# Row sums of the softmax taken from a column of ones beside the values, in a two-layer hybrid attention kernel

## The chip, the cores and the metric

The kernel runs on one core of a Trainium2 chip. The metric is the device time of one execution in microseconds (us); lower is better. The core has a tensor engine (PE, with its weight loads shown as PEld), a vector engine (DVE), a scalar engine (ACT), GpSimd (POOL), and SP, which issues the DMAs. Each engine takes its instructions in order from a queue of its own; semaphores tie the queues together.

## The reference, cut to what matters

Two layers. Each projects the normed input once, runs three kinds of attention on the columns, gates the result and projects it back:

```python
def hybrid_layer(x, ...):
    h = rms_norm(x, g_pre)
    a_q, a_kv, a_g, b_cq, b_ckv, b_kr, c_q, c_kv, z = split_cols(h @ w_in)
    o_a = nsa_attention(...)            # 4 heads: compressed + selected + window 512, sigmoid gates
    o_b = causal_block_attention(...)   # 4 heads, latent keys and values, full causal
    o_c = banded_attention(...)         # 8 heads, window 128, with a sink for each head
    mixed = concatenate([o_a, o_b, o_c]) * silu(z)
    return x + rms_norm(mixed @ w_out, g_post)
```

Every attention is, for each head and each tile of 128 queries, `softmax(q k^T * scale + bias) @ v` with head size 64. The softmax divides by the sum of its row; with sinks, `exp(sink - max)` is added to that sum. There are 1024 tokens, so 8 tiles of queries. With 1024 tokens and 16 blocks of 64, the selected attention selects every block, so the kernel computes it as causal attention.

## The kernel before, in words

Arithmetic: float32 operands are carried as two float16 parts, hi and lo, and a product of two such operands is three float16 matmuls, listed in `HL` as (weights part, values part): (hi, hi), (hi, lo), (lo, hi). `split` makes the parts: an ACT copy for hi (L119), a DVE operation for lo (L120).

Each layer has four stages. `first` makes the keys and values of the banded heads (`L.V`, filled at L415) and of the compressed blocks (`L.VM`, in `compressed`). The second runs the banded heads (kind "swa") with the pieces of `second` as filler on the tensor engine; `second` also fills the latent values `L.VB` (L508). The third runs the three branches of the sparse attention (kinds "cmp", "slc", "win"), with the gate columns (L293, L571) as filler. The last, `last_phase`, runs the latent heads (kind "mla") with the output projection (L911).

The work of attention is cut into units (class `Unit`). A unit is one tile of queries of one head (of two heads for swa and cmp). It goes through three steps, a few units apart:

- `score`: matmuls into a PSUM tile psS (L619, L634, L659); a DVE operation `ttr` that adds the bias and takes the row's extreme (L577, tile mx); then `expo` on ACT, in place (L580). `expo` gives `accum_out=sm`, so ACT also writes the row's sum into the tile sm.
- `turn`, one or two units later: the weights are transposed. Early tiles go through the tensor engine (L698) and are split from PSUM. Where `by_dma` holds, they are split first, into a staging buffer of which there is one for slc (written as sz or HT in the trace), one for win (KC), a few for the others, and a DMA transposes them (L167).
- `values`, two to four units later: L710 multiplies the turned weights by the values, three matmuls of 64 columns for each block of 128 keys, into the PSUM tile psO. psO has one buffer, shared by all groups of units.

After the last unit of a group an end step divides. `end_swa` (two units): `es` = exp of sink against max (L722, L723), sum (L724), reciprocal (L726), scale by the constant OSCALE (L727), product with psO (L728) into the place of the tile's queries in QC. `end_win` (five units, six columns: cmp, slc, win of two heads): reciprocal (L735), gates and OSCALE (L736), product (L739), and then two POOL additions (L742, L743), the last into the place of the queries in QA. `end_mla` (four units): L749, L750 and four products (L753) into the gate tile sz.

A layer has 32 swa units with two exponentials each, 16 cmp units with two, and 32 each of slc, win and mla with one: 192 exponentials, 384 in the kernel. It has 16 swa, 16 win and 8 mla end steps: 80 in the kernel.

The code is written for the tile framework, which sets the semaphores, gives a tile its place when the earlier tile with the same tag is released, and places each engine's instructions at build time by a plan of its own. An engine's order is thus not the order of the source: in the trace, one group of 24 filler matmuls of L293 can have the six matmuls of a cmp unit between its third and its fourth. The tag "V" holds `L.V` and, at the end of a layer, one of the two turned mixed tiles (`mts`, L828).

Of the kernel before, what the change touches and what calls it, by code (L numbers as in the profile page):

```python
# [11 lines left out]
F16 = mybir.dt.float16  # L12
F32 = mybir.dt.float32
# [16 lines left out]
OSCALE = 1.0 / (SP * SQ)  # L30
# [38 lines left out]
def rope_rows():  # L69
    """Cosines and signed sines, for four heads of 32 channels and for halves of the tokens."""  # L70
# [20 lines left out]
def trunk(ctx, tc, a, out):  # L91
# [9 lines left out]
    def view(base, off, shape, dtype):  # L101
        """Words off... of a tile, as another shape and type."""
# [22 lines left out]
    class Ring:  # L125
        """Runs of words of a tile, taken in turn."""
# [15 lines left out]
        def done(self):  # L142
            """The oldest run may be written again."""
            self.live.pop(0)
# [5 lines left out]
    # constants  # L150
# [61 lines left out]
    def split_half(l, g, h, hi, lo):  # L212
        """Half of a group of weights as hi and lo parts."""
# [30 lines left out]
    def normed(hT, xt, xn, gpre, t, hl=None):  # L244
        """A tile of tokens, normed, into its place in the transposed h."""
# [18 lines left out]
    def first_norm(hT):  # L264
        """The transposed h of the first layer."""
# [11 lines left out]
    # ------------------------------------------------------------------ pieces of a layer  # L277
# [3 lines left out]
    def project(L, wh, sub, c, p):  # L281
        """512 tokens of 128 channels."""
# [13 lines left out]
    def split_w(l, g, base=None):  # L296
        """A group of weights as hi and lo parts, in a slot of its own or in base."""
# [5 lines left out]
    def parts_of(L, p, scale=SEVAC):  # L303
        """hi and lo parts of 512 columns of p."""
# [5 lines left out]
    def all_parts(L, p, c):  # L310
        """hi and lo parts of both halves of the tokens, once the second is there."""
# [20 lines left out]
    def turned(u, us, v, vs, table):  # L332
        """Rows us of u turned by their partners, rows vs of v."""
# [6 lines left out]
    def latent_tile(L, p, n, xn):  # L340
        """n channels of a tile of tokens, normed but for the gains."""
# [10 lines left out]
    def compress(L, l, w0):  # L352
        """The blocks of k_cmp and of v_cmp, through their small networks."""
# [32 lines left out]
    def compressed(L):  # L386
        """The blocks of k_cmp and of v_cmp, from the hidden layers of their networks."""
        hid, w2 = L.hid, L.w2
        L.KM = sb([128, 2, 64], F16, "KM")
        L.VM = sb([128, 2, 2, 64], F16, "VM")  # L390
        nc.vector.memset(L.VM, 0.0)
        p = ps("T")
# [4 lines left out]
        for half in range(2):  # L397
            r = slice(64 * half, 64 * half + 64)
            split(p[r, 128:192], SQ, L.VM[r, half, 0], L.VM[r, half, 1])

    def first(L, l, wv):
        """Keys and values of the banded heads, and the queries of four heads."""
# [62 lines left out]
    def second(L, l):  # L465
        """The other queries, and what the latents give; pieces, with their time on the tensor engine."""
# [35 lines left out]
        L.VB = sb([128, 2, NT, 256], F16, "VB")  # L502
        for t in range(NT):
# [4 lines left out]
            split(p[:, :256], SEVAC, L.VB[:, 0, t], L.VB[:, 1, t])  # L508
# [45 lines left out]
    def gate_path(L, l):  # L554
        """z, still without its SiLU, to DRAM; the last columns of the later tiles come with the next phase."""
# [19 lines left out]
    # ------------------------------------------------------------------ attention  # L575
# [466 lines left out]
```

## Time and profile before

| | before |
|---|---|
| time, median of 3 runs | 1182.82 us (1179.52 to 1184.2) |
| span of the profiled execution | 1186.3 us |
| instructions in the span | 25317 |
| PE, PEld busy | 86%, 56% |
| DVE, ACT, POOL busy | 65%, 60%, 9% |
| mean granted TensorE clock | 0.966 of full speed |

The span is from the first to the last instruction of one execution, taken with the profiler; what lies around it is not shown. It is 3.5 us over the median of the timed runs. Busy shares are averages over stages. Matmuls are pipelined and each is shown with its whole latency, so a PE shown as busy can still be waiting a little.

### The profile page before, as it was taken

The numbers are of one execution on the slowest core, as the hardware profiler recorded it, in microseconds if no ns is written. First come the engines' busy times: TensorE is split into PE (matmuls) and PEld (weight loads), VectorE is DVE, ScalarE is ACT, GpSimd is POOL, SyncE is SP. The second block draws the span as 40 slices with busy tenths as digits, with TensorE's granted clock in tenths as the row PEclk, the third lists the DMA queues.
The fourth block names the chain that finished last, engine by engine and source line by source line (L and its number), as shares of the span: only waits on it lengthen the run. The fifth ranks groups of instructions, "written<-read, shape, count | busy, mean of one in ns | idle before, by whom it ended". The sixth has DMA issues, their size and how long they took to land.

```text
span 1186.3 us, 25317 instructions
## 1 busy us (share of the span) xinstructions
PE 1023.0 (86%) x9536; PEld 666.9 (56%) x9536; DVE 766.7 (65%) x2268; ACT 707.9 (60%) x1659; POOL 104.7 (9%) x166
## 2 busy tenths in 40 slices
PE   6969898899888887889979989888997888789977
PEld 4535656658666663445645465664685666534443
DVE  6453677746776775678755356766576777757762
ACT  6442675647665678676744256655575667767651
POOL 1000100001100002111100010000010010021010
PEclk9989999999998997999999999999999999889989
DMA  6784475672587786555476436758327876869882
GB/s 241 172 253 115 119 152 111 131 180 66 128 147 134 132 186 201 143 121 129 112 191 186 112 90 130 147 99 176 106 80 138 163 139 128 221 148 187 186 192 89
DMA packets 313498, 174.42 MB, mean 147 GB/s; under 512 B 273580, under 2 KB 289324, under 8 KB 313376
## 3 DMA queue, kind: packets, MB, share of 16 engines
q1 hardware_dynamic: 313376, 172.81, 63.8%
q8 instruction: 75, 1.23, 0.4%
q14 instruction: 47, 0.39, 0.1%
HBM read 76.63 MB, written 21.41 MB: 83 GB/s over the span
## 4 chain that ended last, share of the span: by engine, by line
PE 30%; DMA 14%; DVE 7%; issue 5%; ACT 4%; POOL 2%; SPq 0%; POOLq 0%; ACTq 0%; DVEq 0%
PE psJ L911 11%; PE psJ L286 8%; DMA arena<-sz 4%; PE psJ L293 3%; DMA arena<-ringS 3%; PE psS L659 2%; PE psO L710 2%; DMA V<-ringS 2%; DMA arena<-KC 2%; DMA sz<-gate_rows 1%; PE psT L698 1%; DVE arena L577 1%; DMA ringS<-in_w_out_dram 1%; DVE sz L120 1%; DVE W L120 1%
## 5 line engine op out<-in xcount | busy, mean ns | idle before, releaser
L580 ACT ACTIVATE arena<-arena,mx 128x256 f32<-128x256 f32 (+8 forms) x384 | 226.4, 590 | 88.5 <-DVE mx L577 86.2
L293 PE MATMUL psJ<-W,HT 128*128 128x256 f16 x1920 | 246.1, 276 | 0.8 <-DVE VB L120 0.8
L293 PEld LDWEIGHTS <-HT 128*128 128x128 f16 x2304 | 217.5, 99 | 34.0 <-issue 6.6
L286 PE MATMUL psJ<-HT,W 128*128 128x512 f16 x864 | 198.4, 383 | 12.5 <-DVE R L120 10.6
L710 PEld LDWEIGHTS <-arena 128*128 128x128 f16 x2964 | 122.5, 99 | 80.0 <-DMA arena<-sz 42.1
L710 PE MATMUL psO<-V,arena 128*128 128x64 f16 x2304 | 106.8, 194 | 43.6 <-DMA arena<-sz 33.0
L286 PEld LDWEIGHTS <-W 128*128 128x128 f16 x864 | 83.9, 99 | 107.4 <-DVE R L120 11.5
L577 DVE CUSTOM_DVE_ANT_0 arena<-psS,R 128x64 f32<-128x64 f32 (+4 forms) x192 | 87.3, 465 | 51.9 <-PE psS L659 26.6
L120 DVE SCALAR_TENSOR_TENSOR sz<-arena,sz 128x512 f16<-128x512 f32 (+4 forms) x96 | 76.6, 801 | 45.5 <-ACT sz L119 44.6
L119 ACT ACTIVATE sz<-arena 128x512 f16<-128x512 f32 (+4 forms) x96 | 68.4, 717 | 39.6 <-DMA arena<-sz 38.4
L659 PE MATMUL psS<-KA,QA 128*128 128x512 f16 (+3 forms) x384 | 80.6, 315 | 1.5 <-DVE mx L577 1.2
L577 DVE CUSTOM_DVE_ANT_0 arena<-psS,arena,nsink 128x256 f32<-128x256 f32 (+1 forms) x128 | 57.9, 461 | 22.2 <-PE psS L634 21.3
L580 ACT ACTIVATION_READ_ACCUMULATOR arena<-arena,mx 128x1 f32 x384 | 72.3, 188 | 0.0
L911 PEld LDWEIGHTS <-arena 128*128 128x128 f16 x384 | 37.9, 104 | 57.7 <-DMA arena<-ringS 11.9
L911 PEld LDWEIGHTS <-V 128*128 128x128 f16 x384 | 36.7, 100 | 56.8 <-DMA V<-ringS 14.6
L120 DVE SCALAR_TENSOR_TENSOR arena<-psT,arena 128x128 f16<-128x128 f32 (+3 forms) x144 | 60.8, 431 | 11.7 <-ACT arena L119 10.7
L120 DVE SCALAR_TENSOR_TENSOR W<-ringS,W 128x1024 f16<-128x1024 f32 x48 | 58.5, 1222 | 14.8 <-ACT W L119 14.4
L698 PE MATMUL psT<-ident,arena 128*128 128x128 f32 x300 | 57.9, 288 | 11.5 <-ACT arena L580 10.0
L659 PE MATMUL psS<-KB,QB 96*128 96x512 f16 (+3 forms) x288 | 60.2, 337 | 2.5 <-DVE mx L577 2.5
L119 ACT ACTIVATE arena<-psT 128x128 f16<-128x128 f32 (+3 forms) x144 | 53.5, 384 | 14.8 <-PE psT L698 12.5
L171 POOL TENSOR_TENSOR rs<-rs,halfneg 128x1 f32<-128x1 f32 x48 | 26.4, 550 | 396.3 <-DVE rs L170 285.0
L911 PE MATMUL psJ<-R,arena 128*128 128x512 f16 x192 | 52.9, 432 | 9.2 <-DMA arena<-ringS 9.2
(152 smaller groups left out, 1598.7 us busy)
## 6 DMA issues: line engine op xcount, KB each, us to landing
ringS<-in_w_in_dram SPq DMA_DIRECT2D x40, 512.0 KB, 4.6
gate_rows<-sz SPq DMA_DIRECT2D x32, 256.0 KB, 3.6
ringS<-in_w_out_dram SPq DMA_DIRECT2D x16, 512.0 KB, 7.2
sz<-gate_rows SPq DMA_DIRECT2D x16, 512.0 KB, 4.2
R<-in_x_dram SPq DMA_DIRECT2D x8, 512.0 KB, 4.4
ringS<-in_cmp_w_dram SPq DMA_DIRECT2D x8, 512.0 KB, 4.8
x<-in_rope_dram SPq DMA_DIRECT2D x8, 512.0 KB, 6.2
x<-in_x_dram SPq DMA_DIRECT2D x8, 512.0 KB, 3.8
```

The source lines that it names most:

```text
L119: nc.scalar.activation(hi, src, AF.Copy, scale=scale)
L120: nc.vector.scalar_tensor_tensor(lo, src, scale, hi, op0=OP.mult, op1=OP.subtract)
L171: nc.gpsimd.tensor_tensor(dst, dst, half_neg[:, :n], op=OP.pow)
L286: nc.tensor.matmul(p, w[:, x, k, sub * 128:(sub + 1) * 128], L.hT[:, y, k, c * 512:(c + 1) * 512], start=(k == 0 and i == 0), stop=(k == K ...
L293: nc.tensor.matmul(p, L.hT[:, y, k, t * 128:(t + 1) * 128], w[:, x, k, :width], start=(k == 0 and i == 0), stop=(k == KT - 1 and i == 2))
L577: nc.vector.tensor_tensor_reduce(o, i0, i1, -alpha, init, OP.add, OP.min, acc)
L580: nc.scalar.activation(b, b, AF.Exp, bias=mx, scale=-1.0, accum_out=sm)
L659: nc.tensor.matmul(p[:, :n], q, k[:, k0 * 128:k1 * 128], start=(i == 0), stop=(i == len(pairs) - 1))
L698: nc.tensor.transpose(p[:, i * 128:(i + 1) * 128], u.b[:, (g + i) * 128:(g + i + 1) * 128], ident)
L710: nc.tensor.matmul(g["O"][:, key * 64:(key + 1) * 64], u.pt[:, x, i, :], v[:, y], start=(key not in seen and j == 0), stop=(last[key] == n ...
L911: nc.tensor.matmul(p, g["mt"][:, x, k], wo[k // 2][:, w, k % 2, cs], start=(k == 0 and i == 0), stop=(k == KT - 1 and i == 2))
```

## The change

`expo` no longer has `accum_out`, and the tile sm is gone. Every head's 64 values get a 65th column: the hi part holds the constant SQ (16) there, so the product with the weights gives the row's sum times SP times SQ, the same scale as the other 64 columns. The sums are read from psO. The (hi, lo) matmul keeps 64 columns; the other two have 65. Outputs of the heads now begin 65 words apart in psO. The column is set by POOL in `L.V` (three memsets of 8 elements a partition) and `L.VB` (four), right after the tile is taken, and by DVE in `L.VM` (two memsets); `split` then writes the values through a pattern with pitch 65. In the end steps the constant OSCALE falls away. The rest of the diff drops docstrings and comments.

```diff
-        L.VM = sb([128, 2, 2, 64], F16, "VM")
+        L.VM = sb([128, 2, 2, 65], F16, "VM")
         nc.vector.memset(L.VM, 0.0)
+        for half in range(2):
+            nc.vector.memset(L.VM[64 * half:64 * half + 64, half, 0, 64:], SQ)
...
+    def ones_of(v, n):
+        for k in range(n):
+            nc.gpsimd.memset(v[:, 0, :, 65 * k + 64:65 * k + 65], SQ)
...
-        L.V = sb([128, 2, NT, 192], F16, "V")
+        L.V = sb([128, 2, NT, 195], F16, "V")
+        ones_of(L.V, 3)
...
-            split(p[:, :192], SEVAC, L.V[:, 0, t], L.V[:, 1, t])
+            v = L.V[:, :, t].rearrange("p s (k d) -> p s k d", d=65)[:, :, :, :64]
+            split(p[:, :192].rearrange("p (k d) -> p k d", d=64), SEVAC, v[:, 0], v[:, 1])
...
-        L.VB = sb([128, 2, NT, 256], F16, "VB")
+        L.VB = sb([128, 2, NT, 260], F16, "VB")
+        ones_of(L.VB, 4)
...
-    def expo(b, mx, sm):
-        nc.scalar.activation(b, b, AF.Exp, bias=mx, scale=-1.0, accum_out=sm)
+    def expo(b, mx):
+        nc.scalar.activation(b, b, AF.Exp, bias=mx, scale=-1.0)
...
+    def sums(p, n):
+        v = p[:, :65 * n].rearrange("p (k d) -> p k d", d=65)
+        return v[:, :, :64], v[:, :, 64]
...
                 for j, (x, y) in enumerate(HL):
-                    nc.tensor.matmul(g["O"][:, key * 64:(key + 1) * 64], u.pt[:, x, i, :], v[:, y],
+                    n_ = 65 - y
+                    nc.tensor.matmul(g["O"][:, key * 65:key * 65 + n_], u.pt[:, x, i, :], v[:, y, :n_],
...
         def end_swa(u):
-            nc.vector.tensor_add(sm, sm, e)
-            nc.vector.reciprocal(rc[:, :4], sm)
-            nc.vector.tensor_scalar(rc[:, :4], rc[:, :4], OSCALE, None, op0=OP.mult)
+            nc.vector.scalar_tensor_tensor(rc[:, :4], e, SP * SQ, sm, op0=OP.mult, op1=OP.add)
+            nc.vector.reciprocal(rc[:, :4], rc[:, :4])
...
         def end_win(u):
-            nc.vector.reciprocal(rc, g["sm"])
-            nc.vector.scalar_tensor_tensor(rc, rc, OSCALE, L.G[:, u.qt, 3 * h0:3 * h0 + 6], op0=OP.mult, op1=OP.mult)
+            o, sm = sums(g["O"], 6)
+            nc.vector.reciprocal(rc, sm)
+            nc.vector.tensor_tensor(rc, rc, L.G[:, u.qt, 3 * h0:3 * h0 + 6], op=OP.mult)
...
         def end_mla(u):
-            nc.vector.reciprocal(rc[:, :4], g["sm"][:, :4])
-            nc.vector.tensor_scalar(rc[:, :4], rc[:, :4], OSCALE, None, op0=OP.mult)
+            o, sm = sums(g["O"], 4)
+            nc.vector.reciprocal(rc[:, :4], sm)
```

## Rows read from the trace of the kernel before

**Rows 1.** The busy time of the engines over the span, from the first part of the page.

```profile
PE 1023.0 (86%) x9536; PEld 666.9 (56%) x9536; DVE 766.7 (65%) x2268; ACT 707.9 (60%) x1659; POOL 104.7 (9%) x166
```

**Rows 2.** The span cut into stages: start and end, length, then busy us and instructions of PE, PEld, DVE, ACT, POOL, the granted clock, the DMA share and GB/s. In order: swa, sparse and last stage of the first layer, the same of the second.

```profile
115.00:259.00 144.00, 127.45 (x1186) 84.01 (x1185) 100.02 (x332) 87.44 (x261) 8.79 (x16) 0.99 0.63 134
259.00:447.00 188.00, 161.99 (x1997) 127.51 (x1996) 132.89 (x444) 125.76 (x330) 18.37 (x32) 0.98 0.66 135
447.00:611.00 164.00, 143.40 (x1083) 79.99 (x1082) 114.04 (x291) 108.95 (x190) 23.19 (x30) 0.95 0.59 147
...
692.00:842.00 150.00, 131.95 (x1199) 86.28 (x1197) 101.36 (x338) 89.37 (x268) 8.79 (x16) 0.97 0.60 129
842.00:1027.00 185.00, 160.10 (x2002) 126.52 (x2000) 133.36 (x445) 126.50 (x329) 18.90 (x32) 1.00 0.68 142
1027.00:1186.30 159.30, 130.78 (x923) 64.76 (x922) 91.78 (x245) 89.63 (x145) 20.45 (x24) 0.90 0.72 161
```

**Rows 3.** What PE waited for over the whole span: total us, times, longest.

```profile
PE psO L710 <- DMA arena<-sz: 33.0, 31, 2.5
...
PE psT L698 <- ACT arena L580: 10.0, 9, 2.6
PE psO L710 <- DMA arena<-KC: 9.3, 13, 1.8
...
PE psS L619 <- POOL QA L743: 6.2, 10, 1.1
...
PE psS L634 <- DVE QC L728: 1.9, 2, 1.0
...
PE psO L710 <- DVE sz L753: 0.9, 1, 0.9
...
PE psO L710 <- DVE QC L728: 0.3, 2, 0.2
PE psO L710 <- DVE tmp L739: 0.3, 1, 0.3
```

**Rows 4.** ACT in order of time, in the sparse stage of the second layer: start, length, instruction.

```profile
926.65 0.33 ACT L580 ACTIVATE arena<-arena,mx 128x64 f32<-128x64 f32 x1
926.88 0.19 ACT L580 ACTIVATION_READ_ACCUMULATOR arena<-arena,mx 128x1 f32 x1
926.98 0.33 ACT L580 ACTIVATE arena<-arena,mx 128x64 f32<-128x64 f32 x1
...
931.52 0.94 ACT L580 ACTIVATE arena<-arena,mx 128x768 f32<-128x768 f32 x1 [0.93 <-DVE mx L577]
932.37 0.18 ACT L580 ACTIVATION_READ_ACCUMULATOR arena<-arena,mx 128x1 f32 x1
932.58 0.84 ACT L119 ACTIVATE sz<-arena 128x768 f16<-128x768 f32 x1
```

**Rows 5.** Groups of one shape on ACT: count, busy us, mean ns.

```profile
L580 ACT ACTIVATION_READ_ACCUMULATOR arena<-arena,mx 128x1 f32 x384 | 72.3, 188 | 0.0
```

**Rows 6.** Pieces of the chain that ended last which lie on L580, the first and the last that hold an accumulator read; "x4" is two exponentials with their reads. The chain is shown back to 459.7 us.

```profile
694.65 0.88 ACT arena L580 x4
...
1031.21 0.61 ACT arena L580 x2
```

**Rows 7.** Groups of one shape on DVE: the end steps, and the same kind of operation with an input in PSUM and without.

```profile
L753 DVE SCALAR_TENSOR_TENSOR sz<-psO,rc,sz 128x64 f32<-128x64 f32 x64 | 14.4, 276 | 5.3 <-ACT sz L885 3.0 <-PE psO L710 2.2
...
L735 DVE RECIPROCAL rc<-sm 128x6 f32<-128x6 f32 x32 | 6.0, 188 | 4.0 <-ACT arena L580 3.8
...
L736 DVE SCALAR_TENSOR_TENSOR rc<-rc,G 128x6 f32<-128x6 f32 x32 | 5.5, 171 | 0.7
L727 DVE TENSOR_SCALAR rc<-rc 128x4 f32<-128x4 f32 x32 | 5.3, 166 | 0.5
...
L724 DVE TENSOR_TENSOR sm<-sm,es 128x4 f32<-128x4 f32 x32 | 4.9, 154 | 3.3 <-ACT es L723 3.3
...
L335 DVE TENSOR_TENSOR tmp<-psJ,x 128x512 f32<-128x512 f32 x4 | 2.8, 692 | 0.4
...
L337 DVE TENSOR_TENSOR tmp<-tmp 128x512 f32<-128x512 f32 x4 | 2.7, 685 | 0.0
```

**Rows 8.** Two groups of PE: the products with the values, and the only matmuls of 65 columns, whose moving rows lie 65 elements apart.

```profile
L710 PE MATMUL psO<-V,arena 128*128 128x64 f16 x2304 | 106.8, 194 | 43.6 <-DMA arena<-sz 33.0 <-DMA arena<-KC 9.3 <-ACT arena L119 0.3
...
L381 PE MATMUL psJ<-R,arena 128*128 128x65 f16 x192 | 6.4, 194 | 0.0
```

**Rows 9.** All engines in order of time around the end of a group in the sparse stage, tile 4 of the second layer.

```profile
911.16 0.56 DVE L739 TENSOR_TENSOR tmp<-psO,rc 128x384 f32<-128x384 f32 x1 [1.02 <-PE psO L710]
...
911.80 0.97 POOL L742 TENSOR_TENSOR tmp<-tmp 128x128 f32<-128x128 f32 x1 [9.00 <-DVE tmp L739]
...
912.85 0.45 POOL L743 TENSOR_TENSOR QA<-tmp 128x128 f32<-128x128 f32 x1
...
913.36 0.23 PE L619 MATMUL psS<-KM,QA 128*128 128x64 f16 x2 [1.14 <-POOL QA L743]
```

**Rows 10.** PE and DVE in order of time around the end of another group of that stage.

```profile
949.78 0.60 PE L293 MATMUL psJ<-W,HT 128*128 128x256 f16 x4
950.50 0.33 PE L710 MATMUL psO<-VM,arena 128*128 128x64 f16 x6
...
949.90 0.55 DVE L739 TENSOR_TENSOR tmp<-psO,rc 128x384 f32<-128x384 f32 x1
```

**Rows 11.** The border between the layers: the last product that reads the turned tile in V, the first write of the second layer's values, and POOL.

```profile
609.46 2.75 PE L911 MATMUL psJ<-W,V 128*128 128x512 f16 x12
...
614.55 0.32 ACT L119 ACTIVATE V<-psJ 128x192 f16<-128x192 f32 x1
...
615.27 0.55 POOL L923 TENSOR_TENSOR rs<-rs,halfneg 128x1 f32<-128x1 f32 x1 [13.18 <-DVE rs L922]
619.59 0.55 POOL L171 TENSOR_TENSOR rs<-rs,halfneg 128x1 f32<-128x1 f32 x1 [3.77 <-DVE rs L170]
```

**Rows 12.** Groups of one shape: a copy to strided and one to contiguous places on ACT, then memsets on POOL and DVE.

```profile
L119 ACT ACTIVATE R<-psJ 64x256 f16<-64x256 f32 x16 | 6.2, 386 | 9.3 <-DVE R L120 4.6 <-PE psJ L286 4.5
...
L119 ACT ACTIVATE VB<-psJ 128x256 f16<-128x256 f32 x16 | 5.9, 371 | 1.2 <-PE psJ L506 1.2
...
masks.py:197 POOL MEMSET ident<- 128x128 f32 x1 | 0.2, 205 | 0.3 <-POOLq L1032 0.3
...
L391 DVE MEMSET VM<- 128x128 uint32 x2 | 0.3, 165 | 0.0
```

More of the change, by code (lines that the diff above doesn't have):

```diff
@@ L29 @@
 ALPHA_B = 96.0 ** -0.5 / (SQ * SQ)
-OSCALE = 1.0 / (SP * SQ)
 NC_CMP = T // 16 - 1
@@ L398, in compressed @@
             r = slice(64 * half, 64 * half + 64)
-            split(p[r, 128:192], SQ, L.VM[r, half, 0], L.VM[r, half, 1])
+            split(p[r, 128:192], SQ, L.VM[r, half, 0, :64], L.VM[r, half, 1, :64])
+    def ones_of(v, n):
+        for k in range(n):
+            nc.gpsimd.memset(v[:, 0, :, 65 * k + 64:65 * k + 65], SQ)
     def first(L, l, wv):
@@ L507, in second @@
                                  start=(k == 0), stop=(k == 2))
-            split(p[:, :256], SEVAC, L.VB[:, 0, t], L.VB[:, 1, t])
+            v = L.VB[:, :, t].rearrange("p s (k d) -> p s k d", d=65)[:, :, :, :64]
+            split(p[:, :256].rearrange("p (k d) -> p k d", d=64), SEVAC, v[:, 0], v[:, 1])
             yield 0.4
@@ L601, in score @@
                 g["mx"] = sb([128, 8], F32, "mx", 4)
-                g["sm"] = sb([128, 6], F32, "sm", 4)
-            mx, sm = g["mx"], g["sm"]
+            mx = g["mx"]
             qs = slice(qt * 128, (qt + 1) * 128)
@@ L620, in score @@
                     ttr(b[:, r], p[:, r], cm[:, h], ALPHA, BIGF, mx[:, 3 * j:3 * j + 1])
-                    expo(b[:, r], mx[:, 3 * j:3 * j + 1], sm[:, 3 * j:3 * j + 1])
+                    expo(b[:, r], mx[:, 3 * j:3 * j + 1])
                     u.pv.append((0, 3 * j, L.VM[:, j]))
@@ L636, in score @@
                     ttr(b[:, r], p[:, r], L.stC[:, h, 256 - nk:], ALPHA, L.nsink[:, h:h + 1], mx[:, col:col + 1])
-                    expo(b[:, r], mx[:, col:col + 1], sm[:, col:col + 1])
+                    expo(b[:, r], mx[:, col:col + 1])
                     for i in range(nk // 128):
-                        u.pv.append((len(u.pv), col, L.V[:, :, k0 + i, 128:192]))
+                        u.pv.append((len(u.pv), col, L.V[:, :, k0 + i, 130:195]))
                 return
@@ L674, in score @@
                 for k in range(k0, k1):
-                    v = L.VB[:, :, k, h * 64:(h + 1) * 64] if kind == "mla" else L.V[:, :, k, w * 64:(w + 1) * 64]
+                    v = L.VB[:, :, k, h * 65:(h + 1) * 65] if kind == "mla" else L.V[:, :, k, w * 65:(w + 1) * 65]
                     u.pv.append((len(u.pv), col, v))
@@ L682, in score @@
                 init = acc
-            expo(b[:, :c], mx[:, col:col + 1], sm[:, col:col + 1])
+            expo(b[:, :c], mx[:, col:col + 1])
         def turn(u):
@@ L719, in end_swa @@
             h0 = u.h // 4 * 4
-            sm, mx = g["sm"][:, :4], g["mx"][:, :4]
+            o, sm = sums(g["O"], 4)
+            mx = g["mx"][:, :4]
             e = sb([128, 4], F32, "es", 2)
@@ L723, in end_swa @@
             nc.scalar.activation(e, e, AF.Exp)
-            nc.vector.tensor_add(sm, sm, e)
             rc = sb([128, 6], F32, "rc", 3)
-            nc.vector.reciprocal(rc[:, :4], sm)
-            nc.vector.tensor_scalar(rc[:, :4], rc[:, :4], OSCALE, None, op0=OP.mult)
-            nc.vector.tensor_tensor(own(L.QC, h0, 4, u.qt), g["O"][:, :256].rearrange("p (k d) -> p k d", d=64),
+            nc.vector.scalar_tensor_tensor(rc[:, :4], e, SP * SQ, sm, op0=OP.mult, op1=OP.add)
+            nc.vector.reciprocal(rc[:, :4], rc[:, :4])
+            nc.vector.tensor_tensor(own(L.QC, h0, 4, u.qt), o,
                                     rc[:, :4].unsqueeze(2).to_broadcast([128, 4, 64]), op=OP.mult)
@@ L748, in end_mla @@
             rc = sb([128, 6], F32, "rc", 3)
-            nc.vector.reciprocal(rc[:, :4], g["sm"][:, :4])
-            nc.vector.tensor_scalar(rc[:, :4], rc[:, :4], OSCALE, None, op0=OP.mult)
+            o, sm = sums(g["O"], 4)
+            nc.vector.reciprocal(rc[:, :4], sm)
             for h in range(4):
                 s = sz[:, 256 + h * 64:256 + (h + 1) * 64]
-                nc.vector.scalar_tensor_tensor(s, g["O"][:, h * 64:(h + 1) * 64], rc[:, h:h + 1], s,
-                                               op0=OP.mult, op1=OP.mult)
+                nc.vector.scalar_tensor_tensor(s, o[:, h], rc[:, h:h + 1], s, op0=OP.mult, op1=OP.mult)
     BY_DMA = {"cmp": NT, "slc": 3, "win": 3, "swa": 1, "mla": 0}
```

3 lines of the change are left out of this document (1 added, 2 removed).

## The prediction

> **What bounds the kernel now.** I read the engines' busy time first: PE 86% of the 1186.3 us span, DVE 65%, ACT 60% [rows 1]. ACT, which the change relieves, is not the bound on average, so the next view is the span cut by stage [rows 2]. ACT is busiest in the two sparse stages, 125.76 of 188 us and 126.50 of 185 (67 to 68%), where PE has 162 and 160; nowhere does it come above PE. So a saving on ACT counts only where something waits for ACT. The list of PE's waits says where [rows 3]. Its largest entries are the weights that a DMA turns, 33.0 + 9.3 us; those follow ACT indirectly, since ACT and DVE must split the weights before the DMA. ACT's exponential itself stands there with 10.0 us in 9 waits. The end steps stand there too, small so far: L743 on POOL 6.2 us in 10 waits, L728 1.9 and 0.3, L739 0.3, L753 0.9.
>
> In the sparse stage each unit runs in a circle: score on PE, L577 on DVE, the exponential, then on the same ACT queue the split of an earlier unit, the lo part on DVE, the DMA, values on PE, and then PE's next score. The accumulator read stands between an exponential and the split behind it [rows 4]: it is on that circle, but once for a circle of several units.
>
> **What it removes.** There are 384 accumulator reads of 188 ns, 72.3 us of ACT busy time [rows 5]. That is not what ACT's queue gets back. A read starts 0.10 us before its exponential ends, and the next instruction 0.09 us before the read ends: exponential at 926.65, read at 926.88, next exponential at 926.98, which is the first one's end [rows 4]. If the next instruction overlaps an exponential as the read does, it starts about 0.10 us sooner. So the queue gets at most 384 x 0.10 = 38 us, and whoever waits for an exponential gets 0.10 to 0.19 us.
>
> How much of the 38 us reaches the end? Two counts. Along the chain that ended last, between 459.7 us and the end, I find 18 reads, from 694.65 to 1031.21 [rows 6]; 18 x 0.10 = 1.8 us, and as much again for the other half of the 384, which lies before: 3.6 us. By PE's waits: 9 for the exponential at 0.19 = 1.7 us, and 44 (31 + 13) for turned weights [rows 3], of which I give every second one 0.10 us (the split behind a read, as at 932.58 in [rows 4], and not one that found ACT idle): 2.2 us. Together 3.9. I take a gain of 4 us; its bounds are 0 and 38.
>
> Off DVE go L724 (154 ns x 32), L727 (166 x 32) and L750 (x 16); L736 becomes a plain product. They are short and DVE has a third of its time free [rows 1, 7]. Nothing counted.
>
> **What it adds on PE.** Of 3360 matmuls on L710, two in three get one column more. The trace holds 192 matmuls of 65 columns with rows at pitch 65, as the values will lie: 6.4 us / 192 = 33 ns each, and a latency of 194 ns, the same as the 64-column matmul [rows 8], whose own share is 106.8 / 2304 = 46 ns. Zero, then. What these rows do not show is an output that starts at an odd word of PSUM, as every second head's now will.
>
> [...]
>
> **What it moves: the end steps.** This is where a price can come from. Before, the reciprocals read sm, which the exponentials wrote long before the products were done; they were over when the last matmul on psO landed, and only L739, L728 or L753 came behind. Now they read psO. Behind the last matmul come a reciprocal (L735, 188 ns) and a product (about L736, 171) before L739; a sum and a reciprocal (about 171 + 173) before L728; a reciprocal before L753 [rows 7]. With the step between two dependent DVE instructions I set 0.43, 0.43 and 0.22 us. DVE is in order, so the next unit's L577 and lo part queue behind; POOL's L742 and L743 start later by as much; and psO, which has one buffer, is released later for the next group's first product.
>
> Reading PSUM instead of SBUF I cost at nothing: the same product of 512 columns takes 692 ns with psJ as an input and 685 with SBUF alone [rows 7]. [...] The rows show 7 ns, and go into the sum.
>
> Who waits? In 10 cases PE waits for L743 already [rows 3], as at 913.36, where L739, L742 and L743 follow each other and PE stands 1.14 us [rows 9]: 10 x 0.43 = 4.3 us. Five more waits are for L728 (four) and L739 (one): 5 x 0.43 = 2.2; one for L753: 0.2. Sum 6.7 us. The bounds are 0, where the planner puts filler matmuls into the gap, and all 80 groups: 32 x 0.43 + 32 x 0.43 + 16 x 0.22 = 31 us. I take half of 6.7, that is 3.3 us, since in the later tiles PE goes on to wait for turned weights, and a PE that comes later waits less there.
>
> **What else it adds.** Fourteen POOL memsets of 8 elements; the nearest row is 128x128 in 205 ns, so under 3 us on an engine that is 9% busy [rows 1, 12]. In the second layer the first three come when the last product has read the old tile of tag V, at about 612 us; POOL is idle from there to 615.27, and the first write of V comes at 614.55 [rows 11]. Three of about 0.2 us fit. If the plan puts them behind POOL's L923 or L171 instead, that write and the second pair of input products wait until 615.9 or 620.2: up to 5 us, once. Four DVE memsets, each below the 165 ns of [rows 12], are under 0.7 us, in a stage with DVE free. The splits of V and VB write with gaps: the strided copy takes 386 ns, the contiguous one 371 [rows 12]; 32 x 15 ns = 0.5 us, beside PE work.
>
> **The sum.** 1186.3 - 4.0 + 3.3 = 1185.6 us of span. The timed median stands 3.5 us below the profiled span, so 1182.1 us; I say 1182.
>
> **The rivals.**
>
> - *ACT's queue is what paces the sparse stage.* For: the split of the weights starts right behind a read [rows 4], and PE loses 42 us waiting for what follows it [rows 3]. Against: ACT is a third idle there [rows 2], and of the waits of the exponential many are for DVE (0.93 us at 931.52). If all 192 reads of the sparse stages counted, 19 us less and 3.3 more: 1167; half of it gives about 1176.
> - *psO held longer paces PE instead.* Where the next group's product sits right behind L739, the 0.43 us fall on PE. In [rows 10] L739 ends at 950.45 and the next group's first matmul starts at 950.50, though the four filler matmuls before it had begun at 949.78; PE's list of waits does not count this, since a matmul's latency covers the gap. If all 32 sparse groups pay, 13.8 us less 4: 1193. It decides from the point where the filler before the next product is shorter than 0.43 us of PE. The stall at the border of the layers would add 5.
> - *The odd starts in PSUM cost.* If they make the write of every second head take as long again, 1680 x 33 ns = 56 us on PE: 1235. [...]
> - *A new plan.* Instructions are placed at build time, so other orders on all engines can shift the time by some us either way. It widens each case and has no sign.
>
> **How the numbers follow.** About 0.5% (5.9 us) is what a measurement of this kernel can tell from no change. The forecast, gain and price that nearly cancel, 0.39, with 1177 to 1188 as its own range. ACT as the pace, in part or whole, 0.33; psO or the border as the pace, 0.25; PSUM starts 0.03. Nearly all of the second case lies beyond 0.5%, some of the third does not: faster 0.34, same 0.39, slower 0.27. The range goes to 1167 on the one side and to 1196 on the other (1193 and part of the border's stall), which leaves the full sums of several cases and the PSUM case outside.
>
> **What would show it.** The 384 reads are gone and ACT's busy time falls from 707.9 us by 38 (if overlaps are counted once) to 72. L710 keeps its 46 ns; if it rises, the PSUM rival holds. L735 stands after the last L710 of its group, with DVE idle before it, and L739 about 0.43 us later. PE's waits on L743, L728 and psO grow by less than 7 us, and those on turned weights do not fall by more than 5. If they fall by 15, the first rival was right; if PE's waits on the end steps grow by over 10, the second. The forecast is wrong if the sparse stages change by more than 5 us each.

## The result, and the profile after

The changed kernel takes 1195.74 us (median of 4, 1194.76 to 1197.92) against 1181.87 us of the kernel before on the same chip: a ratio of 1.0122, with a 95% interval of 1.0085 to 1.0159. It is 14 us slower. The two profiled executions are closer, 1193.0 against 1186.3 us of span.

The engines' busy time, to be read against [rows 1]:

```profile
PE 1030.0 (86%) x9536; PEld 671.9 (56%) x9536; DVE 756.2 (63%) x2224; ACT 675.8 (57%) x1275; POOL 98.7 (8%) x180
```

ACT lost its 384 reads and 32.1 us of busy time, DVE 10.5 us, and PE, which bounds the kernel, gained 7. There is less work on ACT and DVE, and the kernel is slower: the loss must lie in the order, in waiting or in the clock.

The span by stage, with the columns of [rows 2], cut as near to the same work as the new order allows (PE's count differs by up to 29 in the last two stages):

```profile
112.40:260.50 148.10, 130.45 (x1185) 85.41 (x1184) 98.81 (x316) 82.39 (x197) 8.73 (x16) 0.97 0.63 130
260.50:446.00 185.50, 160.82 (x1996) 127.06 (x1995) 130.35 (x444) 119.34 (x231) 15.15 (x33) 1.00 0.68 141
446.00:608.70 162.70, 144.16 (x1084) 79.95 (x1083) 112.54 (x285) 105.12 (x161) 22.79 (x34) 0.95 0.55 142
689.00:837.40 148.40, 130.07 (x1199) 85.94 (x1197) 99.91 (x322) 84.28 (x202) 8.73 (x16) 0.98 0.60 131
837.40:1025.70 188.30, 162.74 (x1975) 128.43 (x1973) 127.52 (x434) 116.84 (x227) 16.69 (x34) 0.97 0.66 138
1025.70:1193.00 167.30, 134.21 (x952) 66.49 (x949) 93.52 (x248) 88.45 (x121) 18.98 (x23) 0.88 0.68 154
```

Against [rows 2] the stages changed by +4.1, -2.5, -1.3, -1.6, +3.3 and +8.0 us. The two layers run the same code, yet one swa stage lost 4 and the other gained 2. One profile can't carry more than that: the change is not a fixed price per group, as the kernel now stands.

The three stages that got longer are the three whose granted clock is lower than before (0.99 to 0.97, 1.00 to 0.97, 0.90 to 0.88); in the others it is equal or higher. The four timed runs of the changed kernel had a mean granted clock of 0.961 to 0.965, and the kernel before takes longer at such a clock too: of its 79 runs beside the experiments, the 11 below 0.965 took 1185.6 us in the mean, the 39 at 0.969 and above 1179.0. With 1181 us as the middle of these runs, an estimate is that up to 4 of the 14 us go with the clock. Whether the change itself brings the lower clock is not shown.

What PE waited for (total us, times, longest), against [rows 3]:

```profile
PE psO L725 <- DMA arena<-sz: 29.7, 26, 2.8
...
PE psO L725 <- DMA arena<-KC: 11.4, 12, 2.6
PE psS L633 <- POOL QA L758: 9.2, 16, 1.0
PE psS L673 <- DVE mx L587: 8.9, 8, 3.2
...
PE psO L725 <- DVE sz L768: 2.3, 4, 0.9
...
PE psO L725 <- DVE tmp L755: 1.6, 6, 0.5
```

Here L725 is the former L710, L751 to L755 the former L735 to L739, L758 the former L743. The waits on the end steps grew by 3.0 us (L758), 1.3 (L755) and 1.4 (L768), and those on the swa product (L728, 1.9 and 0.3) are gone; those on turned weights moved by -3.3 and +2.1. PE's longest line of waits on the row maxima grew from 3.7 (L659) to 8.9 (L673), and the output projection's waits on DMA (L911, now L925) from 19.5 to 24.4. Others fell: all rows of the list together make 153 us before and 152 after, so the 14 us can't be read from it. The end steps themselves, with the product on PE (count, busy us, mean ns, idle before):

```profile
L725 PE MATMUL psO<-V,arena 128*128 128x65 f16 x1536 | 109.2, 195 | 41.1 <-DMA arena<-sz 29.7 <-DMA arena<-KC 11.4
L725 PE MATMUL psO<-V,arena 128*128 128x64 f16 x768 | 94.3, 194 | 0.0
...
L751 DVE RECIPROCAL rc<-psO 128x6 f32<-128x6 f32 x32 | 6.2, 193 | 4.7 <-PE psO L725 4.4
...
L752 DVE TENSOR_TENSOR rc<-rc,G 128x6 f32<-128x6 f32 x32 | 5.1, 160 | 0.1
L741 DVE SCALAR_TENSOR_TENSOR rc<-es,psO 128x4 f32<-128x4 f32 x32 | 4.9, 152 | 9.7 <-PE psO L725 9.7
```

The reciprocal and the swa sum now are what waits for PE. Each costs what it did (193 ns against 188 [rows 7]), so a PSUM operand is not dearer here. The matmuls keep their latency of 194 to 195 ns [rows 8].

The pinned runs below keep the order of the kernel before. In their traces the same group can be followed that [rows 10] shows, and that is where the price is seen.

### The profile page after: what moved, and what is told of

It is laid out like the page before. It is cut to its first block, busy times and chain, and to the rows that moved or that the text cites. A ratio compares the mean times of both kernels' runs of the same rounds, so it can differ in the third digit from the quotient of the medians.

```text
span 1193.0 us, 24905 instructions
## 1 busy us (share of the span) xinstructions
PE 1030.0 (86%) x9536; PEld 671.9 (56%) x9536; DVE 756.2 (63%) x2224; ACT 675.8 (57%) x1275; POOL 98.7 (8%) x180
## 4 chain that ended last, share of the span: by engine, by line
PE 41%; DMA 22%; issue 15%; DVE 11%; ACT 7%; POOL 3%; SPq 1%; POOLq 0%; ACTq 0%; DVEq 0%
PE psJ L285 14%; PE psJ L925 10%; DMA arena<-sz 7%; PE psJ L292 6%; DMA arena<-KC 3%; PE psO L725 3%; DMA arena<-ringS 3%; DVE arena L587 2%; PE psS L673 2%; DMA V<-ringS 2%; ACT sz L118 2%; DVE W L119 1%; ACT arena L590 1%; POOL rs L170 1%; PE psJ L541 1%
## 5 line engine op out<-in xcount | busy, mean ns | idle before, releaser
L590 ACT ACTIVATE arena<-arena,mx 128x256 f32<-128x256 f32 (+8 forms) x384 | 220.7, 591 | 117.9 <-DVE mx L587 115.1
L292 PE MATMUL psJ<-W,HT 128*128 128x256 f16 x1920 | 247.0, 277 | 0.0
L292 PEld LDWEIGHTS <-HT 128*128 128x128 f16 x2304 | 218.2, 100 | 31.7 <-issue 3.0
L725 PEld LDWEIGHTS <-arena 128*128 128x128 f16 x2964 | 124.4, 99 | 79.5 <-DMA arena<-sz 37.1
L725 PE MATMUL psO<-V,arena 128*128 128x65 f16 (+1 forms) x2304 | 111.0, 195 | 41.1 <-DMA arena<-sz 29.7
L587 DVE CUSTOM_DVE_ANT_0 arena<-psS,R 128x64 f32<-128x64 f32 (+4 forms) x192 | 87.5, 465 | 58.0 <-PE psS L633 30.0
L119 DVE SCALAR_TENSOR_TENSOR sz<-arena,sz 128x512 f16<-128x512 f32 (+4 forms) x96 | 76.8, 803 | 51.4 <-ACT sz L118 51.0
L673 PE MATMUL psS<-KA,QA 128*128 128x512 f16 (+3 forms) x384 | 80.6, 315 | 1.3 <-DVE mx L587 0.8
L587 DVE CUSTOM_DVE_ANT_0 arena<-psS,arena,nsink 128x256 f32<-128x256 f32 (+1 forms) x128 | 57.8, 462 | 23.1 <-PE psS L648 21.1
L925 PEld LDWEIGHTS <-arena 128*128 128x128 f16 x384 | 37.5, 103 | 58.4 <-DMA arena<-ringS 14.4
L673 PE MATMUL psS<-KB,QB 96*128 96x512 f16 (+3 forms) x288 | 62.8, 346 | 8.1 <-DVE mx L587 8.0
L925 PEld LDWEIGHTS <-V 128*128 128x128 f16 x384 | 36.9, 101 | 56.8 <-DMA V<-ringS 13.7
L119 DVE SCALAR_TENSOR_TENSOR arena<-psT,arena 128x128 f16<-128x128 f32 (+3 forms) x144 | 60.8, 431 | 10.9 <-ACT arena L118 9.9
L119 DVE SCALAR_TENSOR_TENSOR W<-ringS,W 128x1024 f16<-128x1024 f32 x48 | 58.3, 1221 | 11.2 <-ACT W L118 10.8
L925 PE MATMUL psJ<-R,arena 128*128 128x512 f16 x192 | 51.8, 425 | 12.8 <-DMA arena<-ringS 12.8
L925 PE MATMUL psJ<-R,V 128*128 128x512 f16 x192 | 48.8, 407 | 11.6 <-DMA V<-ringS 11.6
```

The lines of the kernel that those rows point to most:

```text
L119: nc.vector.scalar_tensor_tensor(lo, src, scale, hi, op0=OP.mult, op1=OP.subtract)
L292: nc.tensor.matmul(p, L.hT[:, y, k, t * 128:(t + 1) * 128], w[:, x, k, :width], start=(k == 0 and i == 0), stop=(k == KT - 1 and i == 2))
L587: nc.vector.tensor_tensor_reduce(o, i0, i1, -alpha, init, OP.add, OP.min, acc)
L590: nc.scalar.activation(b, b, AF.Exp, bias=mx, scale=-1.0)
L673: nc.tensor.matmul(p[:, :n], q, k[:, k0 * 128:k1 * 128], start=(i == 0), stop=(i == len(pairs) - 1))
L725: nc.tensor.matmul(g["O"][:, key * 65:key * 65 + n_], u.pt[:, x, i, :], v[:, y, :n_], start=(key not in seen and j == 0), stop=(last[key] ...
```

## The experiments

Three theories stood at first. "Order": the planner, given other instructions, chose a worse order. "Ends": the reciprocals behind the last matmul on psO cost. "Columns": the 65-column products cost. To keep the planner out, most runs fix the order of every engine to that of another kernel, by a dependency without a wait from each instruction to its neighbour in that order:

```diff
+        for e, keys in order.items():
+            names = [KEYS[e, k] for k in keys if (e, k) in KEYS]
+            for x, y in zip(names, names[1:]):
+                tc.add_manual_dep(made[y], x, info, reason="order")
```

"Old order" below is the order of the kernel before. Costs in us are the ratio to the kernel before, run on the same chip in the same minutes, times its median of about 1181 us.

**e1, the new instructions in the old order.**

> The instructions of the changed kernel, each engine's order fixed to that of the kernel before (of the end steps, sum, reciprocal and gates stand right in front of their product, and es has four buffers instead of two, since otherwise that order can't be kept). Theory 'order': the 14 us come from the other order that the planner chose for the changed kernel, so here they are gone: 1178 to 1186 us. Theory 'ends': they come from the reciprocals behind the last matmul on psO: 1192 to 1198, as the changed kernel. Theory 'columns' (65-column products, odd starts in PSUM) says 1192 to 1198 too.

Measured: 1191.5, ratio 1.0091 (1.0057 to 1.0126), +10.8 us.

**e2, the old instructions in the new order.**

> The other corner: the instructions of the kernel before, each engine's order fixed to that of the changed kernel (the scale by OSCALE stands right behind the reciprocal). Theory 'order': 1192 to 1200 us, the order alone brings the loss. Theories 'ends' and 'columns': 1178 to 1187.

Measured: 1201.51, ratio 1.0163 (1.0137 to 1.0189), +19.3 us. None of the theories alone gives both corners. Most of the loss stays when the old order is restored (e1), so the instructions cost by themselves. And the new order, made for late ends, is bad for instructions that have none (e2). Whether it is worth anything to its own instructions is not settled: 1.0122 in it, 1.0091 outside it, and the intervals overlap.

**e3, the reads alone.**

```diff
-        nc.scalar.activation(b, b, AF.Exp, bias=mx, scale=-1.0, accum_out=sm)
+        nc.scalar.activation(b, b, AF.Exp, bias=mx, scale=-1.0)
```

> The kernel before in its own order, with accum_out left out: the sums are read from the tile of maxima instead (the softmax's denominators are left out of the computation). It shows the gain of the 384 reads by itself. The prediction's sum: 4 us, so about 1178. The rival 'ACT paces': 10 to 19 us or more, 1163 to 1172. If the reads gave nothing: 1182.

Measured: 1174.28, ratio 0.9936 (0.9914 to 0.9959), -7.6 us. The gain is real (4.8 to 10.2 us) and larger than forecast, but below what a pacing ACT would give. This version leaves out the denominators, and its eight runs had a mean granted clock of 0.971, against 0.968 beside it, so a part may be the clock's.

**e4, late ends and columns, with accum_out kept.** From e1's kernel:

```diff
-        nc.scalar.activation(b, b, AF.Exp, bias=mx, scale=-1.0)
+        nc.scalar.activation(b, b, AF.Exp, bias=mx, scale=-1.0, accum_out=sm)
```

> As e1, but with accum_out back in the exponential (its sums go to a tile that nobody reads): against e1 it shows the reads a second time, against the kernel before the 65 columns and the late ends together. The prediction's sum: +3.3 for the ends and nothing for the columns, 1185. Theories 'ends' or 'columns': the whole of 14 us and the reads' 4 on top, 1196 to 1200.

Measured: 1197.59, ratio 1.0146 (1.0112 to 1.018), +17.3 us. Against e1 the reads give 6.5 us, in line with e3, though both runs have intervals of about 4 us to each side. So the change is -7 and +17.

**e5, the columns alone.** From the changed kernel, and so for each end step:

```diff
-    def expo(b, mx):
-        nc.scalar.activation(b, b, AF.Exp, bias=mx, scale=-1.0)
+    def expo(b, mx, sm):
+        nc.scalar.activation(b, b, AF.Exp, bias=mx, scale=-1.0, accum_out=sm)
...
-            o, sm = sums(g["O"], 6)
+            o, sm = sums(g["O"], 6)[0], g["sm"]
```

> The products with 65 columns, the column of ones, its memsets and psO's pitch of 65 as in the changed kernel, but accum_out kept and the end steps dividing by its sums as before; each engine's order is that of the kernel before. It splits the 17 us that the run with accum_out and late ends lay above the kernel before. Theory 'ends': the columns cost 0 to 3 us, 1182 to 1185. Theory 'columns': they are most of the 17, 1193 to 1198.

Measured: 1182.45, ratio 1.0009 (0.9982 to 1.0035): nothing that can be measured. "Columns" falls. e5 is also the nearest to a control of the pinning: the fixed order and the columns together cost 1.1 us (-2.1 to 4.1). Neither kernel was pinned, as it is, to its own order. The row of its products, mixed shapes on one line:

```profile
L753 PE MATMUL psO<-V,arena 128*128 128x65 f16 (+1 forms) x2304 | 108.8, 194 | 43.9 <-DMA arena<-sz 34.5 <-DMA arena<-KC 8.2
```

108.8 us against the 106.8 of [rows 8], for outputs of which every second head begins at an odd word. Outputs with an odd start were not slowed here: the mean is 194 ns in both.

**e6, the columns and late ends in end_win alone.** From e5's kernel:

```diff
-            o, sm = sums(g["O"], 6)[0], g["sm"]
+            o, sm = sums(g["O"], 6)
```

> As the run with the columns alone, and end_win alone reads its sums from psO behind the last product (the reciprocals of the three end steps get tiles of their own, so that the order can be kept). Theory 'ends': each of 32 groups pays up to 0.43 us, 10 to 14 us above the run with the columns alone; the other 48 end steps are the rest of the 17. The prediction's term: 4.3 us halved, 2 us above. If the swa and latent ends were the cost: 0 to 2 us above.

Measured: 1193.91, ratio 1.0101 (1.0061 to 1.0142); 10.9 us above e5 (5 to 17 by the two intervals), 0.34 us for each of the 32 groups. The other 48 end steps are left with about 5 of e4's 17, which is within the intervals. "Ends" holds.

The traces have the loss where end_win is. Both sparse stages, from the first product with VM to the first with VB, columns as in [rows 2], in e5 and then in e6:

```profile
264.93:443.66 178.73, 154.71 (x1938) 122.50 (x1939) 129.10 (x434) 120.46 (x318) 17.42 (x30) 1.00 0.67 138
834.57:1016.46 181.89, 156.63 (x1933) 122.91 (x1934) 128.04 (x431) 121.28 (x319) 17.44 (x30) 0.99 0.64 134
```

```profile
262.61:446.35 183.74, 157.91 (x1937) 122.78 (x1938) 130.31 (x435) 120.97 (x318) 18.15 (x30) 0.99 0.65 136
839.41:1027.21 187.80, 159.20 (x1933) 123.43 (x1934) 129.34 (x431) 121.02 (x319) 17.80 (x30) 0.98 0.63 130
```

For the same matmuls 360.6 us became 371.5: 10.9 us, with the clock 0.01 lower. PE's waits on the end step, e5 and then e6:

```profile
PE psS L661 <- POOL QA L791: 5.9, 8, 1.1
...
PE psO L753 <- DVE tmp L788: 0.3, 1, 0.3
```

```profile
PE psS L661 <- POOL QA L791: 7.9, 12, 1.1
PE psO L753 <- DVE tmp L788: 7.7, 19, 0.9
```

How a group pays is seen in e4's trace, DVE first, then PE, at the group of [rows 10]:

```profile
947.12 0.19 DVE L783 RECIPROCAL rc<-psO 128x6 f32<-128x6 f32 x1
947.35 0.17 DVE L784 TENSOR_TENSOR rc<-rc,G 128x6 f32<-128x6 f32 x1
947.62 0.56 DVE L787 TENSOR_TENSOR tmp<-psO,rc 128x384 f32<-128x384 f32 x1
948.09 0.34 DVE L614 CUSTOM_DVE_ANT_0 arena<-psS,R,mx 128x128 f32<-128x128 f32 x1
```

```profile
947.02 0.60 PE L319 MATMUL psJ<-W,HT 128*128 128x256 f16 x4
948.32 0.34 PE L753 MATMUL psO<-VM,arena 128*128 128x65 f16 x6 [0.70 <-DVE tmp L787]
```

Before, the four filler matmuls ended at 950.38 and the next group's product began at 950.50. Now the filler ends at 947.62, two DVE instructions stand in front of L787, the former L739 (0.50 us from 947.12 to 947.62), and PE stands for 0.70 us. The row maxima behind (L614, the former L577) come later by as much. From the last matmul of a sparse group to the first of the next, the timeline of PE shows 1.48 us in mean over 32 groups before and 1.82 in e4 (1.47 in e5, 1.80 in e6): 0.34 x 32 = 10.9 us, the size of e6's loss, though e6's interval is too wide for so close a match to mean much. e4's waits name it, where [rows 3] has 6.2, 0.3 and 0.3:

```profile
PE psS L661 <- POOL QA L790: 8.2, 12, 1.1
PE psO L753 <- DVE tmp L787: 8.2, 18, 0.9
...
PE psO L753 <- DVE QC L773: 3.0, 6, 0.6
```

The whole list is hardly longer than before (154 us and 153), since the waits on turned weights from sz and KC fell from 42.3 us to 35.6: a PE that comes later waits less there.

**e7, psO held longer by dummies.** Is it the hold of psO, of which there is one buffer?

```diff
+            so = g["O"][:, :384].rearrange("p (k d) -> p k d", d=64)[:, :, 63]
+            for i in range(2):
+                nc.vector.tensor_tensor(rc, rc, so, op=OP.mult)
```

> The kernel before in its own order; behind the product of end_swa and of end_win two DVE products of 4 and 6 elements that read psO (into rc, which nobody reads any more), one behind the last product of end_mla. They hold psO 0.3 to 0.4 us longer, and 0.2, and delay neither QC, QA nor sz. If PE waits for psO's release (the prediction's second rival): about as much as the late ends, 8 to 15 us, 1190 to 1197. If the cost of late ends runs through QA, QC and sz, or through a DVE that stands waiting: 1182 to 1185.

Measured: 1196.72, ratio 1.0134 (1.0097 to 1.017), +15.8 us, as the theory of the hold had it. From one sparse group to the next PE takes 1.82 us here too. But these dummies also lengthen DVE's queue; e17 takes that apart.

**e8, end steps cut in two.**

```diff
-            nc.vector.reciprocal(rc, sm)
-            nc.vector.tensor_tensor(rc, rc, L.G[:, u.qt, 3 * h0:3 * h0 + 6], op=OP.mult)
...
+            for x, y in ((0, 5), (5, 6)):
+                nc.vector.reciprocal(rc[:, x:y], sm[:, x:y])
+                nc.vector.tensor_tensor(rc[:, x:y], rc[:, x:y], L.G[:, u.qt, 3 * h0 + x:3 * h0 + y], op=OP.mult)
+                nc.vector.tensor_tensor(t.rearrange("p (k d) -> p k d", d=64)[:, x:y], o[:, x:y],
+                                        rc[:, x:y].unsqueeze(2).to_broadcast([128, y - x, 64]), op=OP.mult)
```

> The changed kernel in the order of the kernel before, with each end step cut: five of end_win's six columns (two of end_swa's four) get sum, reciprocal, gates and product of their own, which can run before the last unit's products are done; each head of end_mla has its own reciprocal. Behind the last matmul stand then a reciprocal and gates of one column and a product of 64 columns instead of 384. Theory 'ends': nothing is added behind the last matmul, so the reads' gain of 7 us stays and perhaps some more: 1170 to 1178. If the 160 added DVE instructions or the columns cost: 1182 to 1192.

Measured: 1219.44, ratio 1.0325 (1.0288 to 1.0361), +38 us. The premise failed; DVE of this run at one group:

```profile
940.38 0.20 DVE L786 RECIPROCAL rc<-psO 128x5 f32<-128x5 f32 x1 [1.83 <-PE psO L752]
940.61 0.17 DVE L787 TENSOR_TENSOR rc<-rc,G 128x5 f32<-128x5 f32 x1
940.88 0.49 DVE L788 TENSOR_TENSOR tmp<-psO,rc 128x320 f32<-128x320 f32 x1
941.29 0.16 DVE L786 RECIPROCAL rc<-psO 128x1 f32<-128x1 f32 x1
941.48 0.44 DVE L787 TENSOR_TENSOR rc<-rc,G 128x1 f32<-128x1 f32 x1
941.96 0.23 DVE L788 TENSOR_TENSOR tmp<-psO,rc 128x64 f32<-128x64 f32 x1
```

The part for the five early columns waited for the last unit's product too (PE's last 15 matmuls on psO begin at 939.72), so six instructions, 1.81 us, stand behind the last matmul in place of the 0.55 us of L739. It looks like a larger dose of the same thing, and the cost is larger; the 160 added DVE instructions were not priced apart.

**e9 to e12, two buffers for psO,** taken from psS or from psT, with a free planner:

```diff
-    BUFS = {"S": 3, "T": 2, "O": 1, "J": 2}
+    BUFS = {"S": 2, "T": 2, "O": 2, "J": 2}
```

> The kernel before with two buffers for psO and two, not three, for psS; the planner is free. The level is open, since psS is short of a buffer: 1175 to 1215. It is the base for the next run.

> The changed kernel with the same buffers. Theory 'psO held longer': with a second buffer the next group needn't wait for the release, so the late ends cost little and the reads' gain of 7 us remains: 3 to 9 us under the run with the old instructions and these buffers. If the late ends cost through QA, QC, sz or DVE: 8 to 17 us over it.

> The kernel before with two buffers for psO and one, not two, for psT; the planner is free. Only the first tiles turn their weights through psT, so less may be lost than with psS: 1175 to 1205. The base for the next run.

> The changed kernel with the same buffers as the run before this one. Theory 'psO held longer': 3 to 9 us under that one; otherwise 8 to 17 us over it. If psT's lost buffer costs under 5 us, this is also a kernel that is faster than both.

Measured: e9 1190.04 (ratio 1.007), e10 1190.5 (1.0069), e11 1206.8 (1.0191), e12 1213.98 (1.0258). With psS short of a buffer the change is even (0.5 us in the medians), with psT short it costs 7: neither -3 to -9 nor +8 to +17. A free plan on both sides leaves this pair open.

**e13, the same pair without the planner:** e10's instructions in e9's order.

> The instructions of the changed kernel with two buffers for psO and two for psS, each engine's order fixed to that of the run with the old instructions and these buffers (1190.0 us; the end steps' sum, reciprocal and gates right in front of their product). It takes the planner out of the pair of runs with two psO buffers. Theory 'psO held longer': the late ends cost 0 to 3 us here against 17 with one buffer, the reads give 7: 1183 to 1187. If the late ends cost through QA, QC, sz or a waiting DVE: 1196 to 1202.

Measured: 1201.05, ratio 1.0174 (1.0139 to 1.0208); 12 us above e9 by the ratios. With the reads' 7 the late ends cost about 19 here, with two psO buffers. The theory that the hold of psO is the whole cost falls. PE's waits of e13 no longer hold one on tmp or QC for psO; these are longer instead (in e9: 7.5 in 12, 4.6 in 8):

```profile
PE psS L700 <- DVE mx L614: 9.5, 20, 1.5
...
PE psS L660 <- POOL QA L789: 8.3, 10, 1.8
```

With one way barred, the delay reaches PE by the row maxima and by QA. psS had one buffer fewer, though, and e9, which has the same two, already waited longer for the maxima: 7.5 us, against 3.7 in the kernel before.

**e14 to e16, psO copied to SBUF first.**

```diff
+            t = sb([128, D], F32, "tmp")
+            ev, t = t[:, 400:790], t[:, :384]
+            nc.vector.tensor_copy(ev, g["O"][:, :390])
+            o, sm = sums(ev, 6)
```

> The changed kernel in the order of the kernel before, one buffer for psO; each end step first copies psO as a whole to SBUF (one DVE copy of 390 or 260 columns, estimated 0.5 and 0.35 us from the products of 384 and 256), and sums, reciprocals and products read the copy. psO is then held about as long as before, but tmp, QA, QC and sz come 0.5 to 0.9 us later, and DVE works some 30 us more. Theory 'psO held longer': the reads' gain is kept but for a few us: 1175 to 1181, faster than both kernels. If the cost runs through QA, QC, sz or DVE: 1195 to 1210.

> The same instructions as in the run before, but the planner is free to order them. Theory 'psO held longer': 1172 to 1184, the plan adding some us either way.

> The kernel before in its own order with accum_out and early reciprocals, and the copy of psO to SBUF in front of each product: psO is held 0.1 us shorter in end_win and end_swa and 0.7 us shorter in end_mla, the results come 0.4 to 0.5 us later. Theory 'psO held longer': 1176 to 1182. If the later results or DVE's added 30 us cost: 1188 to 1198.

Measured: e14 1217.54 (1.0297, 1.0255 to 1.0338), e15 1203.12 (1.0169, 1.0129 to 1.0209), e16 1200.59 (1.016, 1.013 to 1.019). All three fall on the side of later results and DVE's queue. The copy takes as long as the product, so in end_win and end_swa the hold did not get shorter:

```profile
L774 DVE TENSOR_TENSOR tmp<-tmp,rc 128x384 f32<-128x384 f32 x32 | 17.9, 558 | 1.1
...
L773 DVE COPY tmp<-psO 128x384 f32<-128x384 f32 x32 | 17.8, 556 | 4.5 <-PE psO L737 4.3
```

So at an equal hold, 0.56 us more of DVE behind the last matmul cost 19 us (e16), and another way shows: from one sparse group to the next PE takes only 1.57 us, but its waits on POOL's last addition are 14.3 us, against 6.2 in [rows 3]. The free planner saved 15 of e14's 35 us.

**e17 and e18, dummies that touch nothing,** behind the product and in front of it:

```diff
+            for i in range(2):
+                nc.vector.tensor_tensor(dm[:, :6], rc[:, :6], rc[:, :6], op=OP.mult)
```

> The kernel before in its own order, with dummies that touch neither psO nor any result: behind the product of end_win and of end_swa two DVE products of 6 and 4 elements from rc into a scratch tile, behind the last product of end_mla one; 144 in all, about 0.17 us each, 24 us of DVE. psO, QA, QC and sz come free and ready as before; only what stands behind in DVE's queue (row maxima, lo parts) comes later. Theory 'DVE's queue behind the end step': as the run with dummies that hold psO, 10 to 17 us, 1192 to 1199. Theory 'psO held longer' or 'results later': 0 to 4 us, 1182 to 1186.

> The same 144 dummies, but right in front of the product instead of behind it, where DVE waits for the last matmul on psO (as the reciprocals stood before the change). Theory 'DVE's queue behind the end step': hidden in that wait for the most part, 0 to 6 us, 1182 to 1188. If it is DVE's total time that counts: as the run with the dummies behind.

Measured: e17 1190.7 (1.0083, 1.005 to 1.0117), +9.8 us; e18 1186.85 (1.0048, 1.0019 to 1.0078), +5.7 us. Per us of added DVE work that is 0.24 in front (10.4 + 10.2 + 3.2 = 23.8 us), 0.29 behind (18.8 + 10.1 + 4.6 = 33.5 us) and 0.69 for e7's, behind and on psO (10.3 + 10.1 + 2.5 = 22.9 us). DVE's time has a price of its own here, though DVE is a third idle: e17's can't be put down to psO. From one sparse group to the next PE takes 1.55 us in it, near the 1.48 before and not the 1.82 of e4 and e7; PE's waits on the row maxima, three lines of its list, went from 5.9 us before to 12.6 instead. e18's dummies were not all hidden: L739's product ended 1.05 us after the last matmul of its group, in the mean of the sparse groups, against 0.87 before (1.34 in e4), so a part of its cost is lateness too. The steps from e18 to e17 (4 us) and from e17 to e7 (6 us) point to the place behind the wait and to the hold, but each is about as large as its interval, and e17's dummies came out longer than e7's (last section). How the 17 us divide among psO, DVE's queue and late results stays open.

No version that computes the reference beat the kernel before. e3, which does not compute it, suggests what could: the 384 reads gone with the sums still at hand early.

## Why the prediction was wrong

1. **Reads.** The direction was right, the size low: 4 us forecast, 7.6 and 6.5 measured (e3, e4 against e1). Of the two ways in the sum, e3 bears out one: PE's waits on the exponential fell from 10.0 us to 7.7 (from e4 to e1 they did not: 6.3 and 7.6). The other, turned weights, is not seen: those from sz are 34.1 us against 33.0 [rows 3], those from KC 9.4 against 9.3. ACT's busy time fell by 32 us, 84 ns a read, below the 38 to 72 named. That ACT paces the sparse stage is out by the same waits, and by the 356.4 us that e3's two sparse stages took, cut as in e6, against 360.6 before: 4 us, not 10 to 19.
2. **Columns, PSUM reads.** Both priced at nothing, and both right: e5, and 193 ns with the sums in psO against 188 before. The rival of odd starts is out by e5. That an odd start makes a write take as long again, on which the rival's 1235 and 0.03 stand, was the author's supposition; no run shows it, and e5's products kept their mean of 194 ns, at a ratio of 1.0009 for the whole.
3. **End steps: the step that failed.** The prediction set 0.43 us a group, counted the 16 ends for which PE already waited in [rows 3], and then took half of 6.7: 3.3 us. Measured, late ends with the columns cost 17.3 (13.2 to 21.3), of it 10.9 in end_win. The size per group was right (0.50 us in e4's timeline); the count was not. Many groups whose end step PE did not wait for had no slack to spare either: in [rows 10] the filler ends at 950.38 and L739 at 950.45, just ahead of the next product. By the same timeline the next product began within 0.15 us of L739's end in 15 of the 32 sparse groups before, and in 22 in e4. The reason given for the halving does show in e4 (the waits on turned weights fell from 42.3 us to 35.6), but it does not bring the cost down to 3. The second rival had such groups pay, 13.8 us for the 32 sparse ones. That its 1193 stands 3 us from the result is in part luck: it left out the other 48 end steps, and took 4 us for the reads.
4. **psO as the way.** That rival named psO alone. The time from one sparse group to the next on PE (1.82 us in e4 and e7, 1.55 in e17) bears it out as one way; e13, e16 and e17 show that barring it, or leaving it untouched, does not end the cost.
5. **The signs to watch.** PE's waits on the end steps grew by less than 7 us, and neither sparse stage changed by over 5, as the forecast wanted, and it was wrong all the same. The planner puts filler behind the longer chain: at the same group it placed 17 matmuls of L292 before the next product, and L587 and a split (L119) between reciprocal and product. In the mean of the sparse groups L755 ends 2.13 us after the last matmul, where L739 ended after 0.87:

```profile
947.94 0.19 DVE L751 RECIPROCAL rc<-psO 128x6 f32<-128x6 f32 x1
...
948.33 0.16 DVE L752 TENSOR_TENSOR rc<-rc,G 128x6 f32<-128x6 f32 x1
...
949.42 0.55 DVE L755 TENSOR_TENSOR tmp<-psO,rc 128x384 f32<-128x384 f32 x1
```

```profile
948.29 2.02 PE L292 MATMUL psJ<-W,HT 128*128 128x256 f16 x17
950.15 0.35 PE L725 MATMUL psO<-VM,arena 128*128 128x65 f16 x6
```

That hides the wait here. In the profile of the changed kernel the loss stands in the first swa stage (+4.1 us) and the last (+8.0) instead. That the filler used here is what is missing there was not tried, and both had a lower clock; so the cause is shown in the old order, and that it is the same in the planner's own is inferred from e1, which keeps 10.8 of the 14 us.
6. **New plan, no sign.** It got none in the sum, and the new order cost the old instructions 19 us (e2). For the changed kernel itself the difference to the old order, 4 us, is within the intervals, and no larger than what its lower clock may account for.

## What to carry to other kernels

When a change turns an input that is early into one that is the last to come, price the chain behind that input for every group, not only for those whose wait already shows in the list of waits: the others may have no cover left. Work on an engine that is a third idle was not free here; it cost about 0.24 us per us in front of that engine's wait for the bound one, where not all of it was hidden (e18), and 0.3 to 0.95 behind it (e17, e7, and e6 with 10.9 us for 6.2 + 5.3 us moved). Where a planner orders the instructions, run both sets of instructions in both orders before putting a result down to either.

## What was not expected of the hardware

Small DVE products with two SBUF operands were much longer while POOL ran: e17's dummies of 6 elements, behind the product and beside POOL's additions, took 294 ns in the mean, against 163 in front of it (e18) and 161 at the same place with one operand in PSUM (e7). Of e17's 64, the 32 that overlap an instruction of POOL took 432, the others 155. e17, e18 and e7:

```profile
L778 DVE TENSOR_TENSOR dm<-rc 128x6 f32<-128x6 f32 x64 | 18.8, 294 | 1.1
...
L775 DVE TENSOR_TENSOR dm<-rc 128x6 f32<-128x6 f32 x64 | 10.4, 163 | 1.1
...
L778 DVE TENSOR_TENSOR rc<-rc,psO 128x6 f32<-128x6 f32 x64 | 10.3, 161 | 2.2
```

In e8 the gates of one column, which run beside POOL's first addition, took 422 ns against 166 for five columns just before. What makes these instructions longer is not shown.
